# Two rings of attention carry on into the Fourier layer, whose first loads move forward, and the last radix group stays in SBUF

## The chip, the cores and the metric

The kernel runs as one program on one core of a Trainium2 chip. The metric is the device time of an execution in microseconds (us), lower being better. The engines are named as the profile names them: PE is TensorE (matmuls), PEld its loading of weights, DVE is VectorE, ACT is ScalarE, POOL is GpSimd, and SP is SyncE, which here only issues DMAs. Each engine works through its own instructions in order and waits on semaphores for the others.

## The reference

Two layers are applied to a prompt of 2048 tokens and to a sample of 512, both with 1024 channels, in float32. The first is attention in a window of 128 tokens to either side, with 16 query heads, 4 key heads, a bias and a sink; the second mixes with Fourier transforms. A final norm follows.

```python
def attention_layer(x, g, w_in, w_out, sink, rel_bias):
    h = rmsnorm(x, g)
    z = h @ w_in                      # q, k, v, gate
...
    return x + (o * jax.nn.silu(gate)) @ w_out

def fourier_layer(x, g, w_gate, w_out):
    h = rmsnorm(x, g)
    hg = h.astype(jnp.float32).reshape(b, s, N_FGROUPS, FGROUP_CH)
    f = jnp.fft.fftn(hg, axes=(1, 3), norm="ortho").real
    gate = h @ w_gate
    return x + (f * jax.nn.silu(gate)) @ w_out
```

## The kernel before

**Numbers.** A float32 product is made of three matmuls (`matmul3`, L86 to L88): each operand is a high part, rounded to the type fp32r, and a low part. So each weight and each activation is "split": ScalarE copies the high part (L634) and VectorE subtracts it to get the low part (L635; in `split_T` and `turn` the same with other lines).

**Attention.** Five chunks of 512 tokens, the sample first, then four of the prompt. In a chunk, 69 steps `i` interleave by hand the scores, the softmax, the products with v and, as `fill`, the projections of the next two heads (`qg_proj`; weights `wq`, `wg`) and in the end half of the output projection (`out_proj`, weights `wo`). What is left of a chunk's output projection is the list `tail`; the next stage runs it. Attention has its own tile pool `attn`, whose ring "x" has 4 tiles of 4 KB for each partition: rows of x for the norms, transposed x, and in chunks 1 to 4 the sums of gate weights (`gate_sums`, steps 4, 8, 12 and 16), which POOL computes and writes to DRAM (`sumd`, `b21d`). The normed input h of a chunk lies in the ring "hT" of the pool `main`, 8 tiles of 4 KB. The attention output plus the residual goes to DRAM as `x1d`; in the last chunk the residual rows (`xr`, `xrl`) are loaded and stored from POOL's queue.

**Fourier, start.** The pool `four` has a ring "L" of 24 tiles of 4 KB (`left`), a second pool a ring "R" of 16 (`right`). While the `tail` of the last chunk runs, SP loads eight weight tiles (L811): `w32B` from `w_gate` and `w32T` from `sumd`; ScalarE and VectorE split them into `B11`, `B22`, `T1` and `T2`. ScalarE's queue loads the first two tiles of `x1d`, which are normed (`norms`). The transform matrix `chan_sb` is loaded when the phase begins. Four tiles `w32N`, for `N4` and `T3`, are loaded and split after the first transforms.

**Fourier, gates.** Twenty tiles of 128 tokens are taken in ten pairs. For each pair the transposed tiles (`turn`, PSUM bank `trb`, result `tTb`), sums of them (`sums`, `s1` and `s4`, split to S1 to S4 by `parts`) and the weights make the gate of two tiles in seven products instead of eight (`gates`: W, Z, X on PE, `c` and `c12` in SBUF, `gt` the result, written by POOL to `s2d`). The seventh weight, b21, streams in from DRAM for each pair (`more`). The channel transform (`z`) of the next pair, its transposes and sums are hooked in behind the products of the current pair. After every second pair `combine` adds the four z tiles of its group (`radix4`, L822), and POOL writes the four results to DRAM: group 0 to `gsd`, groups 1 to 4 to `evd` and `odd`.

**Fourier, positions.** `position` multiplies by tables of cosines and sines (`tabs`, tile `tb`), makes two rows of u, and multiplies them by the gates read back from `s2d` (L969; mirrored rows come by an indirect DMA from POOL). `split_T` transposes and splits u (PE `tru`, L645). `finish` multiplies by the output weights `wo` (PSUM `fo`), adds `x2` from `x1d` (L986), norms (L998) and stores the rows (L999). The weights `w_fout` are loaded (L1035) and split in the hooks of the last pair's gates, where the four rows of the sample are also begun; then the prompt's 16 rows follow two at a time, from the groups that are read back from `evd` and `odd` (L1057, L1090).

**Order.** A planner places each engine's instructions by the program's order and its own estimates of when operands are ready; manual order hints (`after`) tie some loads to an instruction of attention. A tile of a ring is handed out again as soon as its last reader is done, so a load into it waits for that reader, and what stands behind the load on its queue waits too.

Of the kernel before, what the change touches and what calls it, by code (L numbers as in the profile page):

```python
# [43 lines left out]
def encoder(  # L44
# [6 lines left out]
    main = ctx.enter_context(tc.tile_pool(name="main", bufs=1))  # L51
    wstack = ctx.enter_context(ExitStack())
# [18 lines left out]
    evd = dram.tile([4, 2, P, D], F32, name="evd")  # L71
# [3 lines left out]
    def bank(name):  # L75
        return psum.tile([P, 512], F32, tag="bank", name=name)

# [34 lines left out]
    stage, res_tile = [], []  # L112
# [6 lines left out]
    def attention_phase():  # L119

        with ExitStack() as es:
# [4 lines left out]
            stage.append(lambda name: ap.tile([P, D], F32, tag="x", bufs=4, name=name))  # L126

            def stats(c):
# [5 lines left out]
                def one(i):  # L134
                    xt = ap.tile([P, D], F32, tag="x", bufs=4, name=f"xs{c}_{i}")
# [23 lines left out]
            def make_h(c, invb):  # L159
# [4 lines left out]
                for k in range(KD):  # L164
# [4 lines left out]
                    else:  # L169
                        xk = ap.tile([P, D], F32, tag="x", bufs=4, name=f"xk{c}_{k}")[:, :640]  # L170
# [328 lines left out]
            def gate_sums(k):  # L499
# [3 lines left out]
                def load():  # L503
                    for r in (k, k + 4):
                        t = ap.tile([P, 2, 512], F32, tag="x", bufs=4, name=f"w32g{r}")
# [4 lines left out]
                def lower():  # L510
                    b21 = rows[1][:, 0]
                    t = ap.tile([P, 2, 512], F32R, tag="x", bufs=4, name=f"wB21_{k}")
# [19 lines left out]

            HB = [(b, j) for b in range(4) for j in range(2)]
# [7 lines left out]
            for c in range(len(CHUNKS)):  # L541
# [19 lines left out]
                for i in range(64 + LAG + AVLAG):  # L561
# [49 lines left out]
    def fourier_phase(tail):  # L611
        with ExitStack() as es:
# [7 lines left out]
            def left(shape, dtype, name):  # L620
                return fp.tile(shape, dtype, align_bytes=LINE, tag="L", bufs=24, name=name)
# [4 lines left out]
            ch = left([P, 2, 2, 256], F32R, "chan_sb")  # L626
            POOL.dma_start(ch, chan)
# [42 lines left out]
            class Pair:  # L670
# [78 lines left out]
            def gates(pr, hooks):  # L749
# [23 lines left out]
                c = left([P, 2, 512], F32, f"c{n}")  # L773
# [32 lines left out]
            def build(k, lower, place):  # L806

                def take(src, *names):
                    w32 = place([P, 2, 512], F32, f"w32{names[0]}_{k}")
                    for half, ap in enumerate(src):  # L810
                        SP.dma_start(w32[:, half], ap)  # L811
                    for w, half in sorted(zip(names, range(2))):
                        wg[w][k] = split(place([P, 2, 512], F32R, f"w{w}_{k}"), w32[:, half])

                if lower:
                    take((sumd[1][k][:, 0], sumd[1][k][:, 1]), "N4", "T3")
                else:
                    take([w_gate[h, r // 2, :, (r % 2) * 512 : (r % 2) * 512 + 512] for h, r in ((0, k), (1, k + 4))], "B11", "B22")
                    take((sumd[0][k][:, 0], sumd[0][k][:, 1]), "T2", "T1")
# [16 lines left out]
            def s2_tile(name):  # L836
                return left([P, D], F32, name)

            def x_tile(name):
                return left([P, D], F32, name)  # L840
# [3 lines left out]

            t = left([P, 2, 512], F32, "xrl")
            res_tile.extend((t[:, 0], t[:, 1]))
# [370 lines left out]
```

## Time and profile before

| | us |
|---|---|
| median of 3 runs | 1725.06 (1722.04 to 1725.29) |
| the profiled execution | 1724.35 |
| its span, first to last instruction | 1722.5 |
| PE busy in the span | 1661.5 |
| DVE busy | 1195.1 |
| ACT busy | 862.8 |
| POOL busy | 383.0 |
| mean granted clock of PE | 0.986 of full speed |

In the profile's span, attention ends at about 1145 us (the last `op` matmul starts at 1145.2), the gates' products end at about 1435, and the prompt's rows run to the end. The busy slices of a page are fortieths of the span, 43 us each. A row of the waits names the waiting instruction, what released it, the sum of the waits in us, how often, and the longest. A row of the groups gives line, engine, operation, output and inputs, shapes and count, then busy us and the mean in ns, then idle time of the engine ahead of them and what ended it. A row of a timeline gives the start in us, the duration, and the same names.

### The profile page before, as it was taken

How to read it: one execution, taken by the hardware profiler on the slowest of the kernel's cores; microseconds unless marked ns; L12 is line 12 of the kernel's file. 1: busy time of each engine (PE TensorE's matmuls, PEld its weight loads, DVE VectorE, ACT ScalarE, POOL GpSimd, SP SyncE). 2: the span in 40 equal slices, each digit the busy share in tenths (PEclk: the TensorE clock that was granted, in tenths of full speed). 3: DMA queues.
4: the chain of work that ended last, by engine and by line, in shares of the span. 5: the costliest groups of instructions: out<-in, count | busy, mean ns of one | idle time of the engine just before them, and what ended most of it. 6: DMA issues, size and time to landing. Idle time of an engine off the chain costs nothing. (4 is left out here: it accounts for less than half of the span.)

```text
span 1722.5 us, 25696 instructions
## 1 busy us (share of the span) xinstructions
PE 1661.5 (96%) x8980; PEld 1421.5 (83%) x8980; DVE 1195.1 (69%) x2814; ACT 862.8 (50%) x1966; POOL 383.0 (22%) x524
## 2 busy tenths in 40 slices
PE   9999899999989999899999999999999996999998
PEld 6877679888878888888888888877888885888886
DVE  5898655888538886378873688648676756888553
ACT  6677524666226664156751566536555534342221
POOL 2467641211303112121112211121111120111100
PEclk9999899999999999999999999999999998999999
DMA  8478776544575444763537734385556568563431
GB/s 308 164 285 316 266 284 217 183 176 162 190 261 183 176 171 148 279 230 129 187 141 277 264 135 146 116 334 194 185 199 229 190 231 327 175 226 120 141 107 49
DMA packets 94030, 348.88 MB, mean 203 GB/s; under 512 B 11292, under 2 KB 21532, under 8 KB 75981
## 3 DMA queue, kind: packets, MB, share of 16 engines
q1 hardware_dynamic: 77148, 275.14, 45.5%
q0 software_dynamic: 16176, 70.27, 10.5%
q10 hardware_dynamic: 576, 1.84, 0.4%
q8 instruction: 72, 1.18, 0.3%
q14 instruction: 58, 0.47, 0.1%
HBM read 269.57 MB, written 77.63 MB: 202 GB/s over the span
## 5 line engine op out<-in xcount | busy, mean ns | idle before, releaser
L404 ACT ACTIVATE S<-S 128x385 f32<-128x385 f32 (+1 forms) x320 | 191.2, 598 | 58.5 <-DVE S L400 57.6
L421 ACT CAST pts<-pt 128x384 fp32r<-128x384 f32 (+1 forms) x320 | 144.3, 453 | 113.2 <-PE pt L420 108.8
L422 DVE TENSOR_TENSOR pts<-pt,pts 128x384 fp32r<-128x384 f32 (+1 forms) x320 | 168.5, 527 | 43.4 <-ACT pts L421 40.6
L400 DVE CUSTOM_DVE_ANT_0 S<-spt,b 128x385 f32<-128x385 f32 (+1 forms) x320 | 168.8, 528 | 34.2 <-PE spt L388 29.7
L388 PE MATMUL spt<-kwin,qab 128*128 128x384 f32 (+1 forms) x640 | 158.8, 330 | 9.1 <-DVE S L400 9.1
L409 DVE TENSOR_SCALAR S<-S 128x384 f32<-128x384 f32 (+1 forms) x320 | 151.7, 474 | 9.1
L420 PE MATMUL pt<-ident,S 128*128 128x128 f32 x896 | 150.7, 274 | 0.6 <-DVE pts L422 0.4
L449 POOL TENSOR_TENSOR o<-o,s 128x256 f32<-128x256 f32 x75 | 55.3, 738 | 430.7 <-DVE o L445 424.4
L388 PEld LDWEIGHTS spt<-kwin,qab 128*128 128x128 f32 x640 | 118.4, 189 | 38.0 <-DVE S L400 12.8
L86 PE MATMUL gp<-h,wg 128*128 128x512 f32 x320 | 137.7, 430 | 0.0
L86 PE MATMUL qp<-h,wq 128*128 128x512 f32 x320 | 137.1, 428 | 0.6 <-ACT wq L100 0.6
L434 PEld LDWEIGHTS av<-pts,v 128*128 128x128 f32 x896 | 126.6, 189 | 11.5 <-DVE pts L422 0.2
L434 PE MATMUL av<-pts,v 128*128 128x256 f32 x896 | 135.2, 285 | 0.0
L86 PE MATMUL op<-wo,uT 128*128 128x512 f32 x320 | 126.9, 399 | 2.9 <-DVE xr L484 2.8
L420 PEld LDWEIGHTS pt<-ident,S 128*128 128x128 f32 x896 | 114.1, 141 | 16.3 <-DVE pts L422 4.3
L86 PE MATMUL fo<-wo,tTu 128*128 128x512 f32 x320 | 126.0, 394 | 1.3 <-ACT wo L634 1.2
L87 PE MATMUL op<-wo,uT 128*128 128x512 f32 x320 | 126.6, 396 | 0.0
L88 PE MATMUL qp<-h,wq 128*128 128x512 f32 x320 | 126.2, 394 | 0.1
L88 PE MATMUL op<-wo,uT 128*128 128x512 f32 x320 | 126.0, 395 | 0.0
L87 PE MATMUL fo<-wo,tTu 128*128 128x512 f32 x320 | 125.3, 392 | 0.7 <-DVE wo L635 0.6
L88 PE MATMUL gp<-h,wg 128*128 128x512 f32 x320 | 125.9, 394 | 0.0
L87 PE MATMUL qp<-h,wq 128*128 128x512 f32 x320 | 125.6, 393 | 0.0
(333 smaller groups left out, 4101.9 us busy)
## 6 DMA issues: line engine op xcount, KB each, us to landing
wq<-wsd SPq DMA_DIRECT2D x32, 1024.0 KB, 4.8
wg<-wsd SPq DMA_DIRECT2D x32, 1024.0 KB, 6.6
wo<-wsd SPq DMA_DIRECT2D x32, 1024.0 KB, 4.8
b<-b21d SPq DMA_DIRECT2D x40, 512.0 KB, 7.3
x<-x1d SPq DMA_DIRECT2D x38, 512.0 KB, 4.1
b<-rowd SPq DMA_DIRECT2D x40, 384.0 KB, 4.2
xs<-in_x_dram SPq DMA_DIRECT2D x23, 512.0 KB, 7.1
s2d<-gt POOLq DMA_DIRECT2D x40, 256.0 KB, 5.7
```

The source lines that it names most:

```text
L86: PE.matmul(out, a[0], b[0], start=start, stop=False, skip_group_check=more)
L87: PE.matmul(out, a[0], b[1], start=False, stop=False, skip_group_check=more)
L88: PE.matmul(out, a[1], b[0], start=False, stop=stop, skip_group_check=more)
L388: PE.matmul(ps[:, 2 + k0 * P : 2 + k1 * P], q, kwin[g][:, part, b * P + k0 * P : b * P + k1 * P], start=part == 0, stop=part == 1,)
L400: DVE.tensor_tensor_reduce(out=s[:, e0:e1], in0=ps[:, 1 + e0 : 1 + e1], in1=st["bias"][:, j, 386 - e1 : 386 - e0][:, ::-1], scale=1.0, sca ...
L404: last_exp[0] = ACT.activation(s[:, e0:e1], s[:, e0:e1], AF.Exp, bias=mn, scale=-1.0, accum_out=den)
L409: DVE.tensor_scalar(s[:, ks], s[:, ks], den, None, ALU.mult)
L420: PE.transpose(ps[:, kb, :], s[:, 1 + kb * P : 1 + (kb + 1) * P], ident)
L421: ACT.copy(hi[:, k0:k1, j, :], ps[:, k0:k1, :])
L422: DVE.tensor_tensor(lo[:, k0:k1, j, :], ps[:, k0:k1, :], f32(hi[:, k0:k1, j, :]), ALU.subtract)
L434: PE.matmul(out, v, pt[:, kb].rearrange("p h q -> p (h q)"), start=kb == k0 and part == 0, stop=kb == k1 - 1 and part == 1,)
L449: eng.tensor_tensor(of, of, res["s"][:, cs], ALU.mult)
```

## The change

The ring "x" of attention becomes a pool of its own, `xp`, which lives to the end of the kernel. In the last chunk, steps 24, 28 and 32 load three `w32B` tiles into it and step 36 the transform matrix; steps 57 to 64 place the residual tile `xrl`, the two first tiles of x1, four `w32T` tiles and the fourth `w32B` into the ring "hT", as the h tiles come free. At the start of Fourier these tiles are split by `take`, steps 1 to 8 of `tail`. `x1`, the sums, `c`, `x2` and the gates read back (`s2`) now use the ring "x", and the ring "L" shrinks from 24 to 20 tiles. The last radix group is no longer written to DRAM and read back: `combine` keeps its four tiles in the ring "R" (`kept`). The loads and the splits of `w_fout` are separate steps at other hooks, the first sample position is computed one hook earlier, its table is requested into the ring "hT", and the turns of its two rows get hooks of their own.

```diff
+    xp = ctx.enter_context(tc.tile_pool(name="xp", bufs=1))
...
-    odd = dram.tile([4, 2, P, D], F32, name="odd")
+    odd = dram.tile([3, 2, P, D], F32, name="odd")
...
+    def xtile(shape, dtype, name):
+        return xp.tile(shape, dtype, align_bytes=LINE, tag="x", bufs=4, name=name)
+
+    def htile(shape, dtype, name):
+        return main.tile(shape, dtype, align_bytes=LINE, tag="hT", bufs=8, name=name)
...
+            def quarters(place, k):
+
+                t = ready["B", k] = place([P, 2, 512], F32, f"w32B_{k}")
+                for half, r in enumerate((k, k + 4)):
+                    after(SP.dma_start(t[:, half], w_gate[half, r // 2, :, (r % 2) * 512 : (r % 2) * 512 + 512]), last_exp[0])
+
+            def ahead():
+
+                def transform():
+                    t = ready["chan"] = xtile([P, 2, 2, 256], F32R, "chan_sb")
+                    after(POOL.dma_start(t, chan), last_exp[0])
+
+                def rows(i):
+                    t = ready["x", i] = htile([P, D], F32, f"x1_{16 + i}")
+                    after(SP.dma_start(t, x1d[SEQ + i * P : SEQ + (i + 1) * P, :]), last_exp[0])
+
+                def sums(k):
+                    t = ready["T", k] = htile([P, 2, 512], F32, f"w32T_{k}")
+                    for half in range(2):
+                        after(SP.dma_start(t[:, half], sumd[0][k][:, half]), last_exp[0])
+
+                def last():
+                    t = htile([P, 2, 512], F32, "xrl")
+                    res_tile.extend((t[:, 0], t[:, 1]))
+
+                quarter = [(lambda k=k: quarters(xtile, k)) for k in range(3)]
+                mine = [last, lambda: rows(1), lambda: rows(0), lambda: sums(0), lambda: sums(1), lambda: sums(2),
+                        lambda: sums(3), lambda: quarters(htile, 3)]
+                steps = dict(zip((24, 28, 32, 36), quarter + [transform]))
+                steps.update(zip(range(57, 65), mine))
+                return steps
...
+                    if c == len(CHUNKS) - 1 and i in AHEAD:
+                        AHEAD[i]()
...
-                return fp.tile(shape, dtype, align_bytes=LINE, tag="L", bufs=24, name=name)
+                return fp.tile(shape, dtype, align_bytes=LINE, tag="L", bufs=20, name=name)
...
-                    self.x[i] = left([P, D], F32, f"x1_{t}")
+                    self.x[i] = xtile([P, D], F32, f"x1_{t}")
...
-                        self.pair = left([P, 2, 512], F32, f"s{i}_{self.n}")
+                        self.pair = xtile([P, 2, 512], F32, f"s{i}_{self.n}")
...
-                c = left([P, 2, 512], F32, f"c{n}")
+                c = xtile([P, 2, 512], F32, f"c{n}")
...
+            split_steps = [("T", k) for k in range(4)] + [("B", k) for k in (3, 0, 1, 2)]
             for i, s in enumerate(tail):
                 s()
-                if i == 1:
-                    for k in range(2):
-                        pairs[0].load(1 - k, ACT)
-                    ACT.dma_start(gb, bass.AP(g1.tensor, g1.offset, [[0, P], [1, D]]))
-                if i in (2, 4):
-                    pairs[0].norms((4 - i) // 2)
-                if i in (3, 4, 5, 6):
-                    build(i - 3, False, left)
+                if i in (3, 5):
+                    pairs[0].norms((5 - i) // 2)
+                if 1 <= i < 9:
+                    w, k = split_steps[i - 1]
+                    take(ready[w, k], k, left, *{"T": ("T2", "T1"), "B": ("B11", "B22")}[w])
...
+                if gi == 4:
+                    kept.extend(r)
+                    return
                 for i in range(4):
                     POOL.dma_start(gsd[i] if gi == 0 else evd[gi - 1, i] if i < 2 else odd[gi - 1, i - 2], r[i])
...
+            def f_load(k):
+                w32f.append(left([P, 2, 512], F32, f"w32f{k}"))
+                SP.dma_start(w32f[k].rearrange("p k c -> p (k c)"), w_fout[k // 4, k % 4])
+
+            def f_split(k):
                 for kk in range(2):
+                    t = left([P, 2, 512], F32R, f"wo{2 * k + kk}")
+                    src = w32f[k][:, kk]
+                    tc.keep_in_program_order(ACT.copy(t[:, 0], src))
+                    DVE.tensor_tensor(t[:, 1], src, f32(t[:, 0]), ALU.subtract)
+                    wo.append((t[:, 0], t[:, 1]))
+
+            def turn_first(i):
+                u, r = first[i]
+                pend.append((split_T(u, f"u{r[0]}", r[2] is not None), r))
+
+            one = sample(1, (2, 3), (xtile, xtile), (xtile, left), htile)
             gates(pairs[-1], {
-                0: [lambda: request(one)],
-                1: [lambda: request(sample(0, (0,)))],
-                2: [lambda: request(sample(2, (1,)))],
-                3: [lambda: fout(0), lambda: fout(1)],
-                4: [lambda: first.extend(position(*early.pop(0))), lambda: fout(2), lambda: fout(3)],
-                5: [lambda: fout(4), lambda: fout(5)],
-                6: [lambda: fout(6), lambda: fout(7)],
+                0: [lambda: f_load(0)],
+                1: [lambda: f_load(1), lambda: early.append(sample(0, (0,), (left,), (xtile,), left))],
+                2: [lambda: f_load(2), lambda: early.append(sample(2, (1,), (left,), (xtile,), left))],
+                3: [lambda: first.extend(position(*one)), lambda: f_load(3)],
+                4: [lambda: f_split(0), lambda: f_split(1)],
+                5: [lambda: turn_first(0), lambda: f_split(2), lambda: f_load(4)],
+                6: [lambda: turn_first(1), lambda: f_split(3), lambda: f_load(5)],
             })
-            pend += [(split_T(u, f"u{r[0]}", r[2] is not None), r) for u, r in first]
-            step(*early)
+            new = [t for p in early for t in position(*p)]
+            for k in (6, 7):
+                f_load(k)
+            for k in range(4, 8):
+                f_split(k)
+            finish(*pend.pop(0))
+            new = [(split_T(u, f"u{r[0]}", r[2] is not None), r) for u, r in new]
+            finish(*pend.pop(0))
+            pend += new
...
-                for a in range(4):
+                for a in range(3):
                     t = zt(f"ev{a}_{i}")
                     SP.dma_start(t, evd[a, i])
                     l.append(t)
+                l.append(kept[i])
...
+                    if a == 3:
+                        l.append(kept[2 + i])
+                        continue
```

More of the change, by code (lines that the diff above doesn't have):

```diff
@@ L110, in load_w @@
         return w[:, 0], w[:, 1]
[L112 removed]
+    stage, res_tile, ready = [], [], {}
     def after(ins, anchor):
@@ L504, in load @@
                     for r in (k, k + 4):
-                        t = ap.tile([P, 2, 512], F32, tag="x", bufs=4, name=f"w32g{r}")
+                        t = xtile([P, 2, 512], F32, f"w32g{r}")
                         src = w_gate[:, r // 2, :, (r % 2) * 512 : (r % 2) * 512 + 512]
@@ L804, in fourier_phase, with take, build @@
             wg = {w: [None] * 4 for w in ("B11", "T1", "T2", "B22", "T3", "N4")}
[L806 to L819, printed above, removed]
+            def take(w32, k, place, *names):
+                for w, half in sorted(zip(names, range(2))):
+                    wg[w][k] = split(place([P, 2, 512], F32R, f"w{w}_{k}"), w32[:, half])
+            def build(k):
+                w32 = right([P, 2, 512], F32, f"w32N_{k}")
+                for half in range(2):
+                    SP.dma_start(w32[:, half], sumd[1][k][:, half])
+                take(w32, k, right, "N4", "T3")
             def tt(out, a, b, op):
@@ L1016, in step, with sample @@
                 pend[:] = new
-            def sample(k1, ids):
+            def sample(k1, ids, g_place, s2_places, tb_place):
+                name, tiles = f"s{k1}", pair(k1, 4, SEQ)
                 gl = []
-                for i in ids:
-                    g = x_tile(f"gl{i}")
+                for i, place in zip(ids, g_place):
+                    g = place([P, D], F32, f"gl{i}")
                     SP.dma_start(g, gsd[i])
                     gl.append(g)
-                return f"s{k1}", 4 * k1, gl[0], gl[1] if len(gl) > 1 else None, pair(k1, 4, SEQ)
+                tb = table(name, 4 * k1, tb_place)
+                s2s = [gated(name, r, place) for r, place in zip(tiles, s2_places)]
+                return name, 4 * k1, gl[0], gl[1] if len(gl) > 1 else None, tiles, (s2s, tb)
```

61 lines of the change are left out of this document (27 added, 34 removed).

## The prediction

> **What bounds the kernel now.** I read the page's busy shares and slices first, then the busy time by stretches around the two stage changes, then what ended the waits there, then the queues' timelines.
>
> ```profile
> PE 1661.5 (96%) x8980; PEld 1421.5 (83%) x8980; DVE 1195.1 (69%) x2814; ACT 862.8 (50%) x1966; POOL 383.0 (22%) x524
> PE   9999899999989999899999999999999996999998
> ```
>
> TensorE is the bound: 1722.5 - 1661.5 = 61 us of the span are all that it idles. The slices that fall to 6 and 8 lie at gates to position transform; slice 26, attention to Fourier, still rounds to 9, so finer stretches are needed (columns: stretch and its length, then busy us of PE, PEld, DVE, ACT, POOL, then clock, DMA share, GB/s).
>
> ```profile
> 1144.00:1152.00 8.00, 4.78 (x30) 3.52 (x28) 8.00 (x13) 4.85 (x9) 2.09 (x4) 1.00 1.04 409
> 1152.00:1156.00 4.00, 4.00 (x21) 3.90 (x21) 2.88 (x5) 0.60 (x1) 0.12 (x1) 0.57 1.05 415
> 1160.00:1172.00 12.00, 8.54 (x29) 5.89 (x28) 11.60 (x20) 10.60 (x21) 0.00 (x0) 0.86 0.40 149
> 1300.00:1325.00 25.00, 25.00 (x143) 21.81 (x142) 19.76 (x28) 13.21 (x24) 4.86 (x9) 1.00 0.77 266
> 1420.00:1432.00 12.00, 4.20 (x20) 3.74 (x19) 1.74 (x4) 1.56 (x4) 1.51 (x3) 0.72 1.06 412
> 1436.00:1444.00 8.00, 4.88 (x24) 4.01 (x22) 7.67 (x12) 4.80 (x9) 1.09 (x2) 0.79 0.69 243
> 1448.00:1468.00 20.00, 16.01 (x79) 11.76 (x78) 18.09 (x32) 10.17 (x22) 0.06 (x1) 1.00 0.75 269
> ```
>
> First change of stage: idle 3.22 + 0 + 3.46 = 6.7 us. Clock: 4.00 x 0.43 = 1.7 and 8.54 x 0.14 = 1.2, together 2.9. Ceiling of any gain there: 9.6 us. Second: idle 7.80 + 3.12 + 3.99 = 14.9, clock 4.20 x 0.28 + 4.88 x 0.21 = 2.2: ceiling 17.1. The gates between them have no idle time (25.00 of 25.00), and behind them the slices are at 9. So the change can win about 26.7 us, in these two places.
>
> What ended the waits, first stage change (PE and DVE), then the second:
>
> ```profile
> PE Z L86 <- ACT S L634: 2.5, 1, 2.5
> PE trb L691 <- DVE xr L484: 1.9, 1, 1.9
> PE z L86 <- ACT tTb L693: 1.2, 1, 1.2
> DVE xrl L484 <- DMA xrl<-in_x_dram: 12.9, 1, 12.9
> ```
>
> ```profile
> PE As L86 <- DMA tbs<-in_tabs_dram: 7.8, 1, 7.8
> PE tru L645 <- DVE us L969: 4.4, 3, 2.4
> ```
>
> At the first, VectorE stands 12.9 us for the residual xrl, and then the gate-weight splits crowd out pair 0. At the second one table load stops TensorE for 7.8 us, and then VectorE (18.09 of 20 us) holds it.
>
> **Part 1: loads and splits at the start of Fourier.** The queues' timelines of before:
>
> ```profile
> 982.74 0.58 POOL L527 DMA_DIRECT2D sumd<-w32g  x1 [0.30 <-POOL w32g L497]
> 1126.33 1.33 SPq L811 DMA_DIRECT2D w32B<-in_w_gate_dram  x2
> 1126.51 0.54 POOL L483 DMA_DIRECT2D xrl<-in_x_dram  x1
> 1100.57 9.63 SPq L94 DMA_DIRECT2D wo<-wsd  x2
> DMA  0078003991008700087000780008703830599999
> ```
>
> Sixteen issues on SP (8 tiles, 256 KB each; the first two above), two x1 loads from ScalarE's queue, the transform matrix and two xrl loads from POOL's leave the stretch behind 1124 and are spread over the last chunk. The last row (stretch 1060 to 1135, 40 slices) shows about half of the slices empty before 1124: the loads that go there (3 MB on SP, 0.5 MB xrl) are 9 us at the 409 GB/s of the full stretch. On SP, T1 to T3 and B3 (eight issues) stand between two wo loads that were issued 9.63 us apart; the next wo waits for matmuls, so at 2 MB or 5 us nothing is late. Two of the w32B loads reuse slots of the gate sums, whose last write is the first row (982.7); they come at steps 28 and 32 of the last chunk, when that is long done, so wq and wg behind them on SP wait for nothing. Cost in attention: 0, covered by those empty slices; without that cover 1 to 5 us.
>
> What is freed, by VectorE's groups in 1124 to 1176, and TensorE's output projection (its first and last start):
>
> ```profile
> L635 DVE TENSOR_TENSOR wB<-w32B,wB 128x512 fp32r<-128x512 f32 x8 | 5.2, 685 | 1.6 <-ACT wB L634 1.6
> L635 DVE TENSOR_TENSOR wT<-w32T,wT 128x512 fp32r<-128x512 f32 x8 | 5.2, 685 | 2.6 <-ACT wT L634 2.6
> L88 PE MATMUL op<-wo,uT x64: 387/389/486, 1093.3 to 1145.2; 128*128 128x512 f32 x64
> ```
>
> The 16 splits (10.4 us) move ahead of the output projection's end, into VectorE's 12.9 us wait: started at 1124 to 1130, with two norms of 1.3 us they end at about 1142, before that projection does (1145.6). The evacuations, transposes and pair 0's splits then find VectorE free. Left: the latency of the first transposed tile (1.2 us, the z row) and part of the Z wait, for which I take 1.0 (half of 2.5 less what covers it). New wait: x1_18 goes to the ring slot of pair 0's first sums, so its load waits for S2, some 6 us behind the projection (1151.5, estimated from 16 transposes and four z products), and three of the last four sumd loads stand behind it on SP; 2 MB at 409 GB/s and a landing of a few us put them at about 1159, and their eight splits (0.685 each) end near 1166 to 1168, about when T3 of pair 0, TensorE's sixth product of 2.7 us, needs them. That costs 0 to 2, and I take 0, as they come in the order of need. [...] Gain 9.6 - 2.2 = 7.4 (ends 3, a third, and 9.6).
>
> **Part 2: gates.** Left pool 24 to 20 buffers; x1, the sums and c rotate in three slots (chan holds the fourth).
>
> ```profile
> 1315.81 0.69 DVE L635 TENSOR_TENSOR S<-s,S 128x512 fp32r<-128x512 f32 x1
> 1316.11 0.80 SPq L678 DMA_DIRECT2D x<-x1d  x2
> 1324.53 1.28 DVE L683 SCALAR_TENSOR_TENSOR x<-x,invb,g1b 128x1024 f32<-128x1024 f32 x1 [0.73 <-POOL invb L81]
> 1304.61 1.03 PE L691 MATMUL trb<-ident,x 128*128 128x128 f32 x8
> ```
>
> After the change x1 waits for the last S of the pair before; in before that S ended at 1316.5 and the loads were issued at 1316.1. They shift by under 1 us. The norm ends at 1325.8, the next transposes come one period after 1304.6, at about 1331: 5.4 us of slack. Cost 0.
>
> **Part 3: the last radix group, tables, output weights.** Timelines of POOL and DVE:
>
> ```profile
> 1409.18 0.59 POOL L887 DMA_DIRECT2D odd<-z  x1
> 1415.99 1.08 POOL L928 DMA_DIRECT2D tbs<-in_tabs_dram  x2
> 1417.50 0.69 DVE L788 TENSOR_TENSOR c<-c,Z 128x512 f32<-128x512 f32 x1 [4.18 <-PE Z L88]
> 1465.74 0.69 DVE L986 TENSOR_TENSOR x<-x,fo 128x512 f32<-128x512 f32 x1 [0.33 <-PE fo L88]
> ```
>
> Four POOL writes (odd, evd; 512 KB each) and four SP loads of the same size go: 4 MB, 10 us at 412 GB/s, most of it in the full stretch 1420 to 1432. The first table is issued one pair earlier (before the gate writes of pair 8), so its 7.8 us wait goes. What is late next is VectorE. Its groups in 1424 to 1468:
>
> ```profile
> L635 DVE TENSOR_TENSOR wo<-w32f,wo 128x512 fp32r<-128x512 f32 x16 | 10.3, 684 | 1.1 <-ACT wo L634 1.1
> L652 DVE TENSOR_TENSOR tTu<-tru,tTu 128x512 fp32r<-128x512 f32 x8 | 5.3, 686 | 1.1 <-ACT tTu L651 1.1
> L969 DVE TENSOR_TENSOR us<-us,s2s 128x1024 f32<-128x1024 f32 x4 | 4.8, 1216 | 0.0
> L966 DVE TENSOR_TENSOR us<-ass,Bs 128x254 f32<-128x254 f32 x8 | 3.3, 414 | 10.4 <-PE Bs L88 9.1 <-ACT wo L634 1.2
> L945 DVE TENSOR_TENSOR gs<-gl,gs 128x512 fp32r<-128x512 f32 x4 | 2.6, 683 | 0.0
> ```
>
> In the new order As1 stands straight behind the last B22 product (its sum is taken up at 1417.5), and I take 1421 for VectorE's start on us, after As1, Bs1 and ScalarE's copies. Until the last output weight it has us 4.8 + 3.3 + 3.3 (its second operation, as many), gs 2.6, wo 10.3, half of tTu 2.6, two c and four gt 4.0: 30.9 us, and about 2 us of ping-pong with ScalarE and TensorE: 1454. In before TensorE finished the first sample tile's second half at 1465.6, the same work being done by then. The gain is 11.6, of a ceiling of 17.1; 5.5 us stay (1 to 2 before tru, 3 before As0, the rest before the late wo). Without any cover between VectorE and TensorE the gain is the 7.8 alone; without ping-pong 13.6. POOL's four table loads for the prompt wait for the splits wo9 to wo15, and the power of the first norm is queued behind them; the splits end before that norm is asked for (1454), so 0. The w_fout loads (4 MB) start as weight buffers come free, from pair 9's second product on, before the last B22; 10 us for 4 MB ends before the last wo is needed near 1450: 0.
>
> [...]
>
> **Part 4: the position steps.** x2 and s2 share four slots, so the next x2 load waits until the store of the last x2 in its slot has landed; on SP the next row's store stands behind it.
>
> ```profile
> 1604.63 13.02 SPq L999 DMA_DIRECT2D out_dram<-x  x2
> 1623.33 0.68 DVE L986 TENSOR_TENSOR x<-x,fo 128x512 f32<-128x512 f32 x1
> x<-x1d SPq DMA_DIRECT2D x10, 512.0 KB, 3.5
> out_dram<-x SPq DMA_DIRECT2D x8, 512.0 KB, 2.6
> ```
>
> The store goes at 1604.6, lands 2.6 later, the load 3.5 after that: 1611, for a use at 1623.3. Slack 12 us, cost 0 (two lower rows: the landing times in 1570 to 1680). The s2 load stands behind and has about as much.
>
> **Sum.** 7.4 + 0 + 11.6 + 0 = 19.0. The profiled execution took 1724.35, 0.04% under the median of the three runs: 1724.35 - 19.0 = 1705.3, rounded to 1705, which I give for the median too, as the 0.7 is below what can be told. About 0.2% (3.4 us) is what a measurement of this kernel can tell from no change.
>
> **Rivals.** (a) VectorE stays the bound at both changes: only the table's wait goes, and a third of the first, 7.8 + 3 = 10.8: 1713.5. For it: 8.00 of 8 and 18.09 of 20 us busy there. Against: its 12.9 us of waiting ahead of the first, and 9.1 us of waiting for Bs ahead of the second. (b) Slower: the three-slot ring makes x1 late in every pair. Nine pairs follow; each us beyond the 5.4 of slack costs 9. To undo 19.0 and lose 3.4 more the loads must land 5.4 + 22.4/9 = 7.9 us later than now; at 9 us later the time is 1724.35 - 19.0 + 32.4 = 1738. Against it: the S that they wait for ends when they are issued today. (c) No change: VectorE's stalls reappear where the moved splits land (1124 to 1145, 1417 to 1450) and DMA, at 1.03 to 1.07 of its engines, delivers no earlier; 1724. Against: 4 MB leave for good, and the empty slices. (d) Nearly all goes, the waits being covered: 1699.
>
> **How the numbers follow.** Forecast (1701 to 1709) 0.64; (a) with all between 1709 and 1718 0.17; (d) 0.07; (b) 0.08; (c) 0.04. The range 1698 to 1717 takes in both ceilings (1724.35 - 26.7 = 1697.7) and (a). Faster 0.88, same 0.04, slower 0.08.
>
> **What would show it.** After: no PE wait for tbs; PE idle in the 40 us behind the output projection 2 to 3 us, clock near 1.0 there; VectorE's xrl wait gone and its 16 splits before that point; As1 straight behind the last Z product; PE idle of 5 to 6 us in the 50 us behind it, put down to us, gs and wo; gates at 25.00 of 25. It is wrong if the gates show waits for x1 or c, if wq or wo waits appear in the last chunk, if SP shows long waits for stores in the position steps that end at a late x2, or if the wait for tbs is replaced by one for gs or s2s of the same size.

## The result and the profile after

| | before | after |
|---|---|---|
| median of 4 runs, us | 1725.17 (1722.04 to 1729.75) | 1697.26 (1695.33 to 1699.19) |
| profiled execution, us | 1724.35 | 1698.1 |
| its span, us | 1722.5 | 1696.3 |
| mean granted clock of PE | 0.986 | 0.992 |

The ratio is 0.9836, with a 95% interval of 0.9811 to 0.9861. The change makes the kernel 28 us faster, 26.2 between the two spans, where 19 were forecast; the time is 0.7 us below the low end of the range.

The page of the changed kernel: busy time, and the slices of PE.

```profile
PE 1654.0 (98%) x8980; PEld 1417.4 (84%) x8980; DVE 1193.6 (70%) x2814; ACT 859.0 (51%) x1966; POOL 380.7 (22%) x520
PE   8999899999989999899999999999999999999998
```

PE's idle time in the span is 42.3 us instead of 61. Its busy time fell by 7.5 us with the same 8980 matmuls, and the mean granted clock is 0.992 instead of 0.986. The fall to 6 and 8 in the slices at the second stage change is gone.

Busy time of the changed kernel by stretches (columns as before): the first four are those of before, the last three follow the second stage change, which now begins ten us earlier.

```profile
1144.00:1152.00 8.00, 6.61 (x46) 5.46 (x45) 8.00 (x15) 4.08 (x8) 2.22 (x4) 1.00 0.46 135
1152.00:1156.00 4.00, 4.00 (x33) 3.87 (x32) 3.85 (x7) 3.33 (x7) 0.00 (x0) 1.00 0.77 292
1160.00:1172.00 12.00, 12.00 (x63) 10.11 (x62) 10.98 (x18) 8.94 (x19) 0.55 (x1) 1.00 0.65 239
1300.00:1325.00 25.00, 25.00 (x138) 21.50 (x137) 16.59 (x27) 14.32 (x27) 3.90 (x7) 1.00 0.76 257
1408.00:1428.00 20.00, 19.18 (x102) 15.24 (x100) 17.75 (x32) 12.45 (x28) 2.20 (x4) 1.00 0.78 284
1428.00:1436.00 8.00, 6.57 (x29) 4.98 (x29) 7.36 (x15) 6.83 (x17) 0.54 (x1) 0.79 1.02 415
1436.00:1476.00 40.00, 40.00 (x201) 33.38 (x200) 38.12 (x54) 12.49 (x27) 7.32 (x9) 1.00 0.55 196
```

At the first change of stage 1.4 us of idle time are left and the clock stays at 1.00; at the second 0.8 + 1.4 = 2.2 us, and one stretch at 0.79. The gates have no idle time, as before. What PE still waits for in the changed kernel, at the first and at the second change of stage, and the wait that VectorE now has ahead of the first:

```profile
PE trb L732 <- DVE xr L491: 0.7, 1, 0.7
PE z L95 <- DVE tTb L735: 0.7, 1, 0.7
...
PE fo L93 <- ACT wo L1081: 1.3, 1, 1.3
PE X L93 <- DMA b<-b21d: 0.6, 1, 0.6
...
DVE x L724 <- POOL invb L88: 7.8, 2, 7.4
```

The waits for Z's splits, for the table and for us are gone, and so is VectorE's 12.9 us for xrl; a wait of 7.8 us for a norm's power from POOL has come in its place. It comes before the output projection ends, and PE hardly feels it (experiment 10).

**Where the time came from.** Four marks cut the span: the last `op` matmul (end of attention), VectorE's last sum of c with Z (end of the second kind of product of the last pair), VectorE's second addition to x2 (the first row of the sample is through), and the last `fo` matmul. In us:

| | end of attention | to c | c to x2 | x2 to last fo |
|---|---|---|---|---|
| before | 1145.2 | 272.3 | 48.24 | 249.26 |
| after | 1145.2 | 262.35 | 33.21 | 247.74 |
| gain | 0 | 10.0 | 15.0 | 1.5 |

The gain of 0 in attention is no finer than the mark: over the profiles of all runs the last `op` matmul starts between 1141.4 and 1148.0 us, also where an edit touches nothing before it (1141.4 in experiment 8, 1145.8 in experiment 6; why is open). So the stretches tell more than the totals.

The rows behind these marks, VectorE's timeline of the changed kernel (the rows of before stand in the prediction), with what VectorE does between them:

```profile
1407.55 0.69 DVE L829 TENSOR_TENSOR c<-c,Z 128x512 f32<-128x512 f32 x1 [4.18 <-PE Z L95]
1409.55 0.41 DVE L1006 TENSOR_TENSOR us<-ass,Bs 128x254 f32<-128x254 f32 x1
1418.58 2.49 DVE L1082 TENSOR_TENSOR wo<-w32f,wo 128x512 fp32r<-128x512 f32 x4
1436.42 3.09 DVE L1082 TENSOR_TENSOR wo<-w32f,wo 128x512 fp32r<-128x512 f32 x5
1440.76 0.69 DVE L1026 TENSOR_TENSOR x<-x,fo 128x512 f32<-128x512 f32 x1
```

### The profile page after: what moved, and what is told of

Its sections match the earlier page's. It is cut to its first block, busy times and chain, and to the rows that moved or that the text cites. A ratio compares the mean times of both kernels' runs of the same rounds, so it can differ in the third digit from the quotient of the medians.

```text
span 1696.3 us, 25663 instructions
## 1 busy us (share of the span) xinstructions
PE 1654.0 (98%) x8980; PEld 1417.4 (84%) x8980; DVE 1193.6 (70%) x2814; ACT 859.0 (51%) x1966; POOL 380.7 (22%) x520
## 4 chain that ended last, share of the span: by engine, by line
PE 75%; DVE 10%; DMA 7%; ACT 4%; issue 3%; POOL 1%; SPq 0%; DVEq 0%; POOLq 0%; ACTq 0%
PE av L441 5%; PE spt L395 5%; PE pt L427 5%; PE fo L94 4%; PE fo L93 4%; PE fo L95 4%; PE qp L95 4%; PE qp L93 3%; PE qp L94 3%; PE gp L93 3%; PE gp L95 3%; PE gp L94 3%; PE op L93 3%; PE op L94 3%; PE op L95 3%
## 5 line engine op out<-in xcount | busy, mean ns | idle before, releaser
L93 PE MATMUL gp<-h,wg 128*128 128x512 f32 x320 | 137.8, 430 | 0.0
L441 PEld LDWEIGHTS av<-pts,v 128*128 128x128 f32 x896 | 127.1, 190 | 11.5 <-DVE pts L429 0.2
L93 PE MATMUL fo<-wo,tTu 128*128 128x512 f32 x320 | 126.1, 394 | 1.3 <-ACT wo L1081 1.3
L95 PE MATMUL gp<-h,wg 128*128 128x512 f32 x320 | 125.9, 393 | 0.0
L94 PE MATMUL gp<-h,wg 128*128 128x512 f32 x320 | 125.8, 393 | 0.0
```

The lines of the kernel that those rows point to most:

```text
L93: PE.matmul(out, a[0], b[0], start=start, stop=False, skip_group_check=more)
L94: PE.matmul(out, a[0], b[1], start=False, stop=False, skip_group_check=more)
L95: PE.matmul(out, a[1], b[0], start=False, stop=stop, skip_group_check=more)
L441: PE.matmul(out, v, pt[:, kb].rearrange("p h q -> p (h q)"), start=kb == k0 and part == 0, stop=kb == k1 - 1 and part == 1,)
```

## The experiments

Twelve runs, one of them the changed kernel once more, all against the changed kernel (after, 1697.26 us). They were measured in three later batches; the median of before was 1723.69, 1723.81 and 1722.17 us in these, against 1725.17, so a difference of totals between batches is sure to about 3 us only. Diffs show the changed kernel's lines with a minus. "To c" and "c to x2" are the stretches of the table above, from the profile of each kernel.

**1. The last radix group through DRAM again.**

```diff
-                if gi == 4:
-                    kept.extend(r)
-                    return
...
-                for a in range(3):
+                for a in range(4):
...
-                l.append(kept[i])
```

> The changed kernel, but the last radix group is written to DRAM and read back as before (four writes, four loads of 512 KB); its first table is still requested early. Theory T (the traffic is hidden once the table is ahead of it; VectorE sets the 32 us behind the last gate product): 0 to 3 us over the changed kernel's 1697.3, so 1697 to 1700, no wait for a table, the first sample tile's second half added some 33 us after the last B22 sum, as in the changed kernel. Rival D (the 4 MB themselves are what the second change of stage loses, as DMA is full there): 10 us of transfers come back, of which 5 or more on the path: 1702 to 1707, with TensorE waits for output weights or sample loads.

Measured 1704.96 us (1703.6 to 1706.03), ratio to before 0.9887 (0.9865 to 0.991): 7.7 more than the changed kernel. To c 261.3, c to x2 39.68: the second stretch is 6.5 longer. The longest wait of PE from 1400 to 1450 in this kernel:

```profile
PE X L93 <- DMA b<-b21d: 5.3, 1, 5.3
```

Its busy time by stretches:

```profile
1410.00:1420.00 10.00, 4.68 (x22) 3.58 (x20) 4.46 (x8) 0.00 (x0) 0.00 (x0) 0.89 1.04 415
```

The transfers have a price of their own although the table is early: 4 MB more fill the DMA engines (1.04 of their time, 415 GB/s), and the streamed weight b21 of the last pair, issued on SP at 1400.78, holds PE until 1418.13. In the changed kernel the load is issued at 1401.64, and the same X product starts at 1414.41 after a wait of 0.6. Rival D holds, and theory T's 0 to 3 us is wrong.

**2. The first table requested as late as before, the group kept on chip.**

```diff
-            one = sample(1, (2, 3), (xtile, xtile), (xtile, left), htile)
+            one = sample(1, (2, 3), (xtile, xtile), (xtile, left), None)
...
-                3: [lambda: first.extend(position(*one)), lambda: f_load(3)],
+                3: [lambda: box.append(table("s1", 4, left)), lambda: first.extend(position(*one[:5], (one[5][0], box[0]))), lambda: f_load(3)],
```

> The changed kernel, but the table of the first sample position is requested as late as in the kernel before, behind the other two tables; the last radix group stays on chip. Theory T (the wait for the table was a matter of its place in the queue, and VectorE's work behind it starts by as much later): As waits 3 to 8 us for the table, and the time rises by that and by one clock dip of 1.7 us: 1701 to 1707. Rival D (it was late only because 4 MB stood in front of it): lands in time or up to 2 us late, 1697 to 1699.

Measured 1703.58 us (1702.66 to 1704.44), ratio 0.9879 (0.985 to 0.9907); one execution of four took 5815 us, for no known cause, and is left aside. It is 6.3 slower than the changed kernel, and c to x2 is 41.41, 8.2 longer. PE's two longest waits in 1400 to 1450:

```profile
PE As L93 <- DMA tbs<-in_tabs_dram: 2.9, 1, 2.9
PE As L93 <- ACT gs L984: 2.6, 1, 2.6
```

Busy time by stretches:

```profile
1410.00:1420.00 10.00, 10.00 (x44) 8.86 (x45) 5.00 (x11) 4.57 (x11) 0.00 (x0) 0.70 0.27 112
```

The wait for the table is only 2.9 us here: the tables land 8.5 us after their issue (median of three), against 15.8 in experiment 3, where the 4 MB move too. But the work in its wake starts late (the wait for gs, 2.6 us), and the clock of these ten us is 0.70, which is 3.0 us.

**3. Both undone.** The edits of 1 and 2 together.

> Both: the last radix group goes through DRAM and the first table is requested behind those writes. Both theories expect the wait of the kernel before, 7 to 10 us at As; theory T 1706 to 1711 (the wait, a clock dip, and VectorE late by as much); rival D at least what the traffic alone costs plus the wait, 1709 to 1715. If wait and traffic add up exactly, the two parts are independent.

Measured 1710.41 us (1709.47 to 1714.46), ratio 0.9925 (0.9899 to 0.995). From c to x2 it takes 48.18 us; before took 48.24. PE's longest wait there:

```profile
PE As L93 <- DMA tbs<-in_tabs_dram: 11.5, 1, 11.5
```

So these two edits are the whole second gain, and they add up: 6.5 + 8.2 = 14.7 of the 15.0. The new places of the output weights' loads and splits, which this kernel keeps, give nothing alone; whether the other two edits would be worth as much without them, no run shows. With both undone the tables take 15.8 us to land, and the wait is 11.5.

**4. The first weights and x1 loaded behind attention again** (same tiles and rings; only xrl and the transform matrix stay early; norms and splits one step of the tail later).

```diff
-                steps = dict(zip((24, 28, 32, 36), quarter + [transform]))
-                steps.update(zip(range(57, 65), mine))
+                steps = {36: transform, 57: last}
+                late.extend(quarter + mine[1:])
...
+                if i == 2:
+                    for s in late:
+                        s()
```

> The changed kernel, but the eight weight tiles and the two x1 tiles are loaded only behind the last wo load (about 1126), into the same rings; the residual tile and the transform matrix stay early. Theory T (the first change of stage lost 10 us because the splits came late and crowded out pair 0's work on VectorE): most of the 10 us come back, 1703 to 1708, splits from 1132 on, TensorE waits for transposed tiles and S. Rival X (it was the residual tile that VectorE stood 12.9 us for, in front of the splits): with xrl early the splits follow the loads at once and only 2 to 4 us come back, 1699 to 1702.

Measured 1712.33 us (1709.5 to 1715.55), ratio 0.9931 (0.9904 to 0.9958): 15.1 slower than the changed kernel, all of it in the stretch to c (276.6, against 262.35), which is even 4.3 longer than in before, and more than theory T allowed. The longest wait of VectorE, and two of PE, around the end of attention:

```profile
DVE invb L87 <- ACT jkb L701: 17.7, 1, 17.7
...
PE trb L732 <- DVE xr L491: 4.9, 2, 3.9
PE z L93 <- DVE xr L491: 2.3, 1, 2.3
```

Three stretches of busy time right behind it:

```profile
1148.00:1152.00 4.00, 0.84 (x4) 0.45 (x4) 4.00 (x7) 3.86 (x8) 0.59 (x1) 0.91 0.74 293
1152.00:1156.00 4.00, 1.29 (x5) 0.89 (x6) 4.00 (x8) 4.00 (x9) 0.54 (x1) 0.50 0.34 133
1156.00:1160.00 4.00, 1.66 (x5) 0.84 (x5) 4.00 (x8) 0.25 (x1) 0.38 (x1) 0.50 0.08 22
```

The norm waits 17.7 us for its late x1, in a VectorE order in which evacuations and splits stand behind it; then VectorE is busy in all of the twelve us (4.00 of 4) and PE in 3.8 of them, at half its clock in the last eight. ScalarE's timeline, the rows for the first x1 here and in before:

```profile
1142.57 1.06 ACT L701 ACTIVATE jkb<-x 128x1024 bf16<-128x1024 f32 x1 [18.95 <-DMA x<-x1d]
```

```profile
1131.82 1.06 ACT L660 ACTIVATE jkb<-x 128x1024 bf16<-128x1024 f32 x1 [7.92 <-DMA x<-x1d]
```

So this kernel is not before over again: its x1 stands behind six weight loads on SP and lands 10.8 us later than in before. It shows that splits which begin late (at 1147.8) hold PE, but not whether the weights or x1 are what has to come early.

**5. Only the residual tile xrl late.**

```diff
-                mine = [last, lambda: rows(1), lambda: rows(0), ...
+                mine = [lambda: rows(1), lambda: rows(0), ...
...
+            t = left([P, 2, 512], F32, "xrl")
+            res_tile.extend((t[:, 0], t[:, 1]))
```

> The changed kernel, but the residual tile of the last chunk is again a tile of the Fourier pool and so loaded late, behind the loads of the start; weights and x1 stay early. Theory T (late splits crowd out pair 0): the residual alone blocks VectorE's queue, but the transfers ahead of it are gone, so it lands within 5 us and the splits still end near the output projection's end: 0 to 2 us, 1697 to 1699. Rival X (the residual was the cause): VectorE stands 5 to 13 us, the splits move behind 1145, 3 to 8 us: 1700 to 1705.

Measured 1698.1 us (1696.7 to 1699.21), ratio 0.985 (0.9822 to 0.9877): as the changed kernel. VectorE's longest wait at the end of attention:

```profile
DVE xrl L491 <- DMA xrl<-in_x_dram: 5.7, 1, 5.7
```

The wait for xrl is back with 5.7 us and costs nothing. The 12.9 us of before were not tested at that length, but its trace speaks against them as the cause. ScalarE's timeline of before, the first of the weights:

```profile
1137.77 0.62 ACT L634 CAST wB<-w32B 128x512 fp32r<-128x512 f32 x1 [4.80 <-DMA w32B<-in_w_gate_dram]
```

ScalarE makes the first high part only now, when its load has landed, so VectorE had no split to do before 1138.4, about when its wait for xrl ended (1138.59); at most the first norm could have come sooner. The splits were late because their weights were.

**6. Half of the output weights' low parts computed twice** (the same result; eight more VectorE instructions, 4.8 us).

```diff
-                    DVE.tensor_tensor(t[:, 1], src, f32(t[:, 0]), ALU.subtract)
+                    for _ in range(2 if k >= 4 else 1):
+                        DVE.tensor_tensor(t[:, 1], src, f32(t[:, 0]), ALU.subtract)
```

> The changed kernel with eight of the sixteen low parts of the output weights computed twice (wo8 to wo15), which leaves the result as it is and gives VectorE 8 x 0.60 = 4.8 us more between the second sample position and the end of the first output tile. Theory T (VectorE sets this stretch): 4 to 5 us more, 1701.5 to 1702.5, or more with a clock dip. Rival C (VectorE's work is covered, what is left is latency and the clock): 0 to 2 us, 1697 to 1699.

Measured 1702.47 us (1697.29 to 1703.92), ratio 0.9868 (0.9836 to 0.9901). VectorE's timeline, the two marks:

```profile
1407.46 0.69 DVE L829 TENSOR_TENSOR c<-c,Z 128x512 f32<-128x512 f32 x1 [4.18 <-PE Z L95]
1445.46 0.68 DVE L1026 TENSOR_TENSOR x<-x,fo 128x512 f32<-128x512 f32 x1
```

From c to x2 38.00 us, 4.8 more than 33.21: what is added to VectorE comes out at the end in full. VectorE's queue is what sets this stretch now, as Part 3 said. One of the four executions took only 1697.29 us, as little as the changed kernel; no profile of it was kept, so why is open.

**7. The gate weights' 16 low parts computed twice** ahead of the first transposes (the same result; 9.6 us of VectorE).

```diff
-                    wg[w][k] = split(place([P, 2, 512], F32R, f"w{w}_{k}"), w32[:, half])
+                    t = place([P, 2, 512], F32R, f"w{w}_{k}")
+                    wg[w][k] = split(t, w32[:, half])
+                    if double[0]:
+                        DVE.tensor_tensor(t[:, 1], w32[:, half], f32(t[:, 0]), ALU.subtract)
```

> The changed kernel with the sixteen low parts of the gate weights at the start of Fourier computed twice: 16 x 0.60 = 9.6 us more on VectorE ahead of and at the end of the output projection. Theory T (early loads give VectorE a slack of 5 to 10 us there): 0 to 5 us, the second half of the splits moving past 1145. Rival V (VectorE is still full there, as it is 4 of 4 us busy in 1144 to 1152): the whole 9.6 us, 1707.

Measured 1705.88 us (1705.64 to 1706.16), ratio 0.9895 (0.9868 to 0.9923). The stretch to c is 7.8 longer. PE's longest wait in it:

```profile
PE trb L732 <- DVE xr L491: 6.5, 1, 6.5
```

I had taken VectorE's end at 1142, with some us to spare before the projection's end. It has hardly any: 9.6 us more cost 7.8, nearer to rival V than to theory T. The norm's 7.4 us wait for POOL stands in the middle of the splits and uses the slack up.

**8. Four of the output weights' low parts on POOL**, since VectorE sets that stretch.

```diff
-                    DVE.tensor_tensor(t[:, 1], src, f32(t[:, 0]), ALU.subtract)
+                    (POOL if k >= 4 and kk else DVE).tensor_tensor(t[:, 1], src, f32(t[:, 0]), ALU.subtract)
```

> A try at a faster kernel: the low parts of wo9, wo11, wo13 and wo15 are computed by GpSimd instead of VectorE. VectorE loses 4 x 0.60 = 2.4 us. Theory T: up to 2.4 us faster than the changed kernel, 1695, if GpSimd's 1.5 us each lie beside it; rival C: no change, or slower where TensorE then waits for GpSimd's part (1697 to 1700).

Measured 1701.37 us (1697.31 to 1704.31), ratio 0.9875 (0.9847 to 0.9904): no faster. c to x2 is 35.27, 2.1 longer. A wait of PE that the changed kernel doesn't have:

```profile
PE fo L94 <- DVE wo L1082: 1.0, 2, 0.5
```

Busy time by stretches:

```profile
1430.00:1440.00 10.00, 9.05 (x37) 7.13 (x37) 10.00 (x12) 3.59 (x8) 6.77 (x8) 0.83 1.05 385
```

VectorE is still busy in all ten us (10.00 of 10), beside 6.77 us of POOL. The timelines show where the saving went: VectorE's and POOL's rows of this kernel, and VectorE's row of the changed kernel for a like pair.

```profile
1428.99 3.25 DVE L1082 TENSOR_TENSOR wo<-w32f,wo 128x512 fp32r<-128x512 f32 x2
1428.72 4.66 POOL L1082 TENSOR_TENSOR wo<-w32f,wo 128x512 fp32r<-128x512 f32 x3 [7.18 <-ACT wo L1081]
```

```profile
1432.35 1.29 DVE L1082 TENSOR_TENSOR wo<-w32f,wo 128x512 fp32r<-128x512 f32 x2
```

Two subtractions take VectorE 3.25 us while POOL does the same work, instead of 1.29, and a third 1.11 instead of 0.68: 2.4 us more, which is what the four moved ones would have saved (4 x 0.60).

**9 to 12. The wait for the norm.** The changed kernel once more, as the base of one batch; the norms of the first two tiles behind the 16 splits; that, and the turn of the second sample row behind the output weights; and the doubled splits of 7 with the norms behind them.

```diff
-                if i in (3, 5):
-                    pairs[0].norms((5 - i) // 2)
+                if i in (8, 9):
+                    pairs[0].norms(9 - i)
...
-                6: [lambda: turn_first(1), lambda: f_split(3), lambda: f_load(5)],
+                6: [lambda: f_split(3), lambda: f_load(5)],
...
                 f_split(k)
+            turn_first(1)
```

The changed kernel once more:

> The changed kernel itself, as a yardstick for the other runs on this chip: 1697 within 2 us.

The norms behind the splits:

> The changed kernel with one edit at the start of Fourier: the norms of the first two tiles are asked for behind the sixteen splits of gate weights instead of between them, so VectorE does not stand 7.4 us for GpSimd's power with splits behind it. Theory T (VectorE reaches the end of the output projection just in time, and its queue is what leaves 1.4 us of TensorE idle there): from the projection's last matmul to the last B22 product 260.4 to 261 us instead of 261.85, so 0.8 to 1.4 us less, 1696, too little for the verdict but to be seen in the stretch. Rival L (the 1.4 us are the latency of transposes and copies): the stretch stays at 261.5 to 262.

Norms and turn:

> b2_norm, and the transposes and splits of the mirrored sample row (2051) come behind all output weights instead of between them: 1.2 us less on VectorE ahead of the first output tile's second half. Theory T (VectorE's queue sets that stretch): from the last B22 sum to the second add of the first sample row 31.5 to 32.2 us instead of 33.2, in all 1694 to 1696. Rival C (ScalarE's order or the clock sets it): 33 us or more.

Doubled splits, norms behind them:

> Sixteen gate-weight splits computed twice on VectorE (9.6 us more), with the norms behind them. Theory T (the 7.4 us that VectorE stands for a norm are its whole slack, and they are given back here): the stretch from the projection's end to the last B22 product is 262 to 265 us, against 269.6 with the norms between the splits and 261.85 without the extra work. Rival L (the extra work always costs what it takes): 269 to 271.

| | median, us | ratio to before | to c | c to x2 |
|---|---|---|---|---|
| changed kernel | 1696.93 (1696.05 to 1697.92) | 0.9855 (0.984 to 0.987) | 261.7 | 34.10 |
| norms behind | 1696.67 (1695.63 to 1701.84) | 0.9852 (0.9836 to 0.9867) | 261.0 | 35.50 |
| norms and turn | 1695.89 (1691.56 to 1697.21) | 0.9839 (0.9823 to 0.9854) | 260.6 | |
| doubled, norms behind | 1703.98 (1702.32 to 1706.44) | 0.9901 (0.9886 to 0.9916) | 264.8 | 35.02 |

(With the turn moved, x2's additions come in another order, so its last stretch can't be compared; from c to the last `fo` it takes 281.2 us, the changed kernel 280.95 and 281.8 in its two profiles, so the 1.2 us that theory T gave to the turn don't show. The profile of the kernel with the norms behind is of its slowest execution, in which attention ends at 1148.) Busy time by stretches, the kernel with the norms behind its splits:

```profile
1144.00:1148.00 4.00, 4.00 (x19) 3.32 (x18) 1.59 (x3) 0.00 (x0) 0.59 (x1) 1.00 0.26 100
1148.00:1152.00 4.00, 4.00 (x34) 3.83 (x33) 3.63 (x7) 3.12 (x7) 1.62 (x3) 1.00 0.69 262
1152.00:1156.00 4.00, 4.00 (x35) 4.00 (x34) 3.85 (x7) 3.40 (x7) 0.00 (x0) 1.00 0.02 6
```

PE has no idle time left behind attention's end at 1148 (4.00 of 4), and VectorE is free before it (busy in 1.59 of 4). That is worth about 1 us to c; but this stretch is between 261.3 and 262.5 in the kernels that leave the start of Fourier as it is, and the intervals of the totals can't tell 1 us from nothing. The slack is real all the same: with it the doubled splits cost 264.8 - 261.0 = 3.8 us to c instead of 7.8. In the total only 1.9 of that show against experiment 7 (1703.98 and 1705.88, of different batches); the doubled kernel's profile has a wait of 3.0 for b21 at the second change of stage, and the rest isn't settled. No version here beats the changed kernel by more than can be measured.

## Why the prediction came out too slow

The direction, the two places and VectorE as what bounds the second of them hold. Rival (d), that nearly all of the idle time goes, is what happened; I had given it 0.07. Two terms of the sum were too small: Part 1 by its ceiling, Part 3 by its count of VectorE's work.

**Part 1, forecast 7.4, measured 10.0.** The failing step is the ceiling of 9.6 itself. Busy time of the whole stretch, before and then after:

```profile
1144.00:1184.00 40.00, 32.86 (x166) 26.46 (x165) 33.57 (x54) 27.07 (x50) 3.31 (x6) 0.91 0.63 245
```

```profile
1144.00:1184.00 40.00, 38.61 (x230) 33.61 (x229) 34.34 (x57) 27.34 (x51) 6.70 (x12) 1.00 0.65 224
```

Idle time falls from 7.14 to 1.39, by 5.75. I had 6.7 for before (0.46 lay outside my stretches), and had left 2.2 instead of 1.4. The other 4.2 of the gain are not idle time; most of them are clock (0.91 and 1.00 over these 40 us, so 3.6), where I had 2.9. PE's timeline of before shows, in the z matmuls, what a dip is:

```profile
1153.08 0.41 PE L87 MATMUL z<-chan_sb,tTb 128*128 128x256 f32 x1
...
1156.06 0.28 PE L88 MATMUL z<-chan_sb,tTb 128*128 128x256 f32 x1
```

Most of them last 0.41 us from 1152.44 to 1155.42 and those from 1155.58 on 0.28, and the granted clock is 0.51 in 1152.00 to 1155.40 and 1.00 in 1155.60 to 1160.00: about 3.45 us at half speed from 1151.97 on, which is 1.7 us lost. The second dip costs as much by its clock, 0.72 in 1164 to 1168 and 0.86 in 1168 to 1172. Two dips make 3.4; my second had 1.2, since I multiplied the busy time by a mean that runs over idle time too. So 0.6 to 0.8 stays unexplained. The gaps ahead of the first dip were of 1.9 and 1.2 us. The forecast counted the 2.9 us of clock as won whole; no run shows how short gaps must be for that. The changed kernel's clock was 1.00 over these 40 us with its two gaps of 0.7 us, but experiment 12 had 1.00 there too with a gap of 2.6 us, longer than either gap of before.

The mechanism was right in that splits on VectorE held PE (experiments 4 and 7), and that xrl's wait need not go (5) supports the splits and not the residual. That the weights, and not x1, are what had to come early is read from before's trace and not tested. Wrong was the slack. VectorE's timeline of the changed kernel, the norm in the middle of the splits and the last of them:

```profile
1136.25 1.29 DVE L724 SCALAR_TENSOR_TENSOR x<-x,invb,g1b 128x1024 f32<-128x1024 f32 x1 [7.38 <-POOL invb L88]
...
1142.26 4.30 DVE L676 TENSOR_TENSOR wB<-w32B,wB 128x512 fp32r<-128x512 f32 x7
```

The splits end at 1146.6, not at 1142 and ahead of the projection's end, since I had given the two norms their own 1.3 us and no wait for POOL's power, which is queued behind DMA issues that wait for stores of x1 (2.6 and 3.7 us on POOL, ahead of the power at 1135.63). It cost about 1 us (the norms behind the splits), so the forecast went wrong by little here, but nothing more was free: experiments 7 and 12.

**Part 2, forecast 0:** right, 25.00 of 25. Loads in attention, forecast 0: right as far as the mark tells, the last `op` starts at 1145.2 in both. x1_18 and the late sums, forecast 0: right, 12.00 of 12 in 1160 to 1172.

**Part 3, forecast 11.6, measured 15.0.** The bound was right: VectorE (experiment 6). The failing step is its sum of 30.9 us, made of the durations that the groups show. Four wo instructions in a row take 2.49 us and five 3.09, so one starts every 0.60 us although each is shown as 0.68: 0.08 us of a duration lie over the next instruction. By these spacings the same work is 27.9. VectorE also began on us 2.0 us behind the sum with Z (1409.55 against 1407.55) where I had 3.5; against that, one addition to x2 and one split of tTu (1.3 together) come before the mark and were not in my list. 3.0 + 1.5 - 1.3 = 3.2 of the 3.4 that are missing.

Within the term, its parts were told wrongly too. I gave the table 7.8 us and the 4 MB no price of their own; one by one they are worth 8.2 and 6.5, the latter through a wait of which the forecast had no word, b21's. And the new places of the output weights, part of the change, are worth nothing alone (experiment 3).

**Part 4, forecast 0, measured 1.5.** The position steps took 249.26 us in before and 247.74 after; over the experiments it is 248.7 to 248.8 with the group in DRAM (1 and 3) and 247.5 to 248.5 without it, the one with another order of additions left out. So about 1 us of it may be the reads that left, which lies hardly beyond the spread; the rest is open.

**The sum.** 10.0 + 0 + 15.0 + 1.5 = 26.5, against 26.2 between the spans; the other 0.3 lie behind the last `fo` matmul. Rival (a), VectorE stays the bound and only a third goes, is out, although the row that spoke for it (8.00 of 8 busy) is the same after: VectorE is full there in both, in the changed kernel from 1146.6 on with evacuations and transposes that PE waits for. Rivals (b) and (c) are out by the gates and by the waits.

## What to carry to other kernels

When an engine's queue sets a stretch, count its work by the starts of consecutive instructions (here 0.60 us apart), not by their durations (0.68); and price a gap of TensorE with the slow clock that follows it, where one does: here 1.7 us for each dip of before (the changed kernel's two gaps of 0.7 us at the first change of stage had none, nor had one of 2.6 us in experiment 12). Traffic that is put away can pay through a transfer that had nothing to do with it (here b21's, 5.3 us of PE's wait with the 4 MB and 0.6 without), so ask of a full DMA stretch which streamed load stands in it. The longest wait that a profile shows (12.9 us for xrl) may cost little (at 5.7 us it cost nothing, experiment 5); whether the work behind it in the same queue could have begun sooner decides.

## What the runs showed of the hardware that I had not expected

- One gap of 1.3 us, among 1.43 us of idle time in 1428 to 1436, goes with a clock of 0.79 over those 8 us in the changed kernel (0.50 in 1432 to 1434), that is 1.7 us, as much as a whole dip of before.
- A 512 KB load took from 1400.78 to about 1418 while the DMA engines were 1.04 busy in 1410 to 1420 (experiment 1). The same load, issued at 1401.64, was waited for only until 1414.41 with less traffic (8.51 MB in 1396 to 1425 instead of 9.51), and PE's wait for it varies from nothing to 3.0 us between kernels that do the same there (none in experiment 5, 0.6 and 1.1 in two profiles of the changed kernel, 3.0 in experiment 12).
- POOL and VectorE did not subtract side by side at full pace: two of VectorE's subtractions took 3.25 us beside POOL's, instead of 1.29 (experiment 8).
